# RMS norms' sums and rows moved to VectorE's 32x32 transposes, and half of the last residual turned there

## The chip, the cores and the metric

The kernel runs on one core of one Trainium2 chip. The metric is device time in microseconds (us), the median of three runs. The engines are TensorE (PE, with its weight loads as PEld), VectorE (DVE), ScalarE (ACT), GpSimd (POOL) and SyncE (SP, which here only issues DMAs). DMAs are issued by SP, POOL and ACT.

## What is computed

One hybrid layer on 1024 tokens of width 1024, in fp32:

```python
h = h + 0.5 * rmsnorm(swiglu(rmsnorm(h, ffn1_pre_g), ffn1_w_gu, ffn1_w_down), ffn1_post_g)
h = h + rmsnorm(hybrid_mixer(rmsnorm(h, mix_pre_g), w_in, ..., ssd_norm_g, attn_norm_g, w_out), mix_post_g)
h = h + rmsnorm(memory_cross_attention(rmsnorm(h, xa_pre_g), rmsnorm(mem, mem_g), xa_wq, xa_wkv, xa_wo), xa_post_g)
h = h + 0.5 * rmsnorm(swiglu(rmsnorm(h, ffn2_pre_g), ffn2_w_gu, ffn2_w_down), ffn2_post_g)
```

The mixer joins a stick-breaking attention and a Mamba-2 scan (SSD); the output of the scan is normed in two groups of channels before the output projection. An `rmsnorm` divides each token by the root of its mean square over the channels, and multiplies by a gain for each channel.

## The kernel before, in words

**Layout.** Activations lie with channels on the 128 partitions and tokens along a row. The tokens are two halves `hh` of 512, so a tensor of width 1024 is eight tiles of 128x512 for each half (`d` or `k` counts them). Only the last stage (`down_rows`) has tokens on partitions, since the output is stored so. Large products are split into high and low parts (`xh`, `xl`; `whi`, `wlo`) and done as three matmuls; the two FFNs use seven products of blocks instead of eight (`down7` for the second half of an FFN).

**Stages.** ffn1, the mixer's SSD part, its attention (heads in pairs, `p` from 0 to 7, the next pair's projection `inproj(p + 1)` merged in), `mix_out`, `xattn`, ffn2 with `down_rows` last.

**A norm.** Squares of the eight tiles are added into an accumulator `acc` of 128x512 (channels modulo 128 by tokens). Then the sum over partitions and what follows from it:

- `rms_cols` (L322): for each 128 tokens an fp32 matmul with `acc` as the stationary operand and a column of ones (`small`), into one column of a PSUM bank `ms`; then root (ACT) and reciprocal (DVE). It gives `c`, 128x4, with tokens on partitions. For the two SSD groups (`group_norm`, L1525) it works on the two `yacc` tiles together, for the memory (`keys`, L1548) on `Ct` of 256 columns.
- `rms_rows` (L346): for each of the four columns an fp32 matmul of the column, broadcast, with the identity, which puts each token's factor on all partitions; ACT copies the bank to a tile `r` of 128x512. `cpre`, `cpost`, `cy`, `cmem` are such columns, `rpre`, `rpost`, `rn` such rows.

`post` (L386) norms the output of a block, adds it to the residual `h` (also written to DRAM), and gathers the squares for the next norm; `pre` (L484) is that next norm alone. Some users take `c`, some take `r`, some both. `mix_row` and `memory_values` spread factors in the attention, `norm_row` (L2058) in `mix_out`.

**What sets the order.** A class records the program. `_pe` chains the matmuls in the order of the calls and adds an estimate of each to a `clock`. `later` is a list of steps with due times on that clock; a step due is called between two matmuls. In `pinned(t)` the matmuls float: they are placed behind the matmul at which the clock passes `t`. `kp` keeps an instruction in the order of the program on its engine. Elsewhere a scheduler orders DVE, ACT and POOL by priority, `urgent` raising it. Each engine and each queue works in order. The bank `ms` is one buffer, shared with transposes of the attention (`nb`).

**Attention, first pair.** `steps` (L1715) turns a half of v: DVE transposes, a store to DRAM (`vt`), four loads back (`dv<-vt`, L1731, 32x16x32 elements each). `kevac` stores k's high and low parts into `K` by SP DMAs (`k<-xl`, L1700), and `z<-k,q` multiplies with `K`.

**Last stage.** `down_rows` (L1140) takes eight tiles of the residual for each half (`fetch_h`, L1158, POOL). `shift` (L1160) turns them by 128x128 transposes on PE into two banks `mm`; `end` adds them to the normed result; `store` writes out. For the first half this is `early`, during the fifth and sixth product, for the second it is `last`, at the very end. `ssq` and `gain` gather squares and scale the rows. `blk<-h` (L685) are loads of residual tiles at the start of an FFN, from which DVE and ACT make the block sums (`wc`, `S`, `xl`) of its seven products.

Of the kernel before, what the change touches and what calls it, by code (L numbers as in the profile page):

```python
# [10 lines left out]
F32 = mybir.dt.float32  # L11
# [36 lines left out]
class Kern:  # L48
# [296 lines left out]

    def rms_rows(self, c, r, behind=None):  # L346
# [39 lines left out]
    def post(self, hh, gname, r2, gnext=None, out=None, step=None, spread=True, pins=(23000, 28000), accs=None, at=None, tail=None, hold=False, late=None):  # L386
# [10 lines left out]

        def cols():
            self.rms_cols([accs], c, r2=r2)

        def rows():
            self.rms_rows(c, r)
# [25 lines left out]
        if out is None:  # L428
            self.h[hh] = [self.tc.dram_tile([P, H], F32, name=self.nm(f"h{hh}{d}")) for d in range(KT)]
# [12 lines left out]
        if step is None:  # L442
            with self.pinned(T0 + t1):
                cols()
            with self.pinned(T0 + t2):
                rows()
# [19 lines left out]
        if out is None:  # L466
# [4 lines left out]
            self.held = [lambda: self.rms_cols([accs2], c2)]  # L471
            if not hold:
                q.append((t + t1, self.held.pop()))
            if spread:
                q.append((t + t2, lambda: self.rms_rows(c2[:, :], r2_)))
# [8 lines left out]
    def pre(self, hh, accs, t1, t2):  # L484
        c = self.t(self.rp, [P, 4], F32, f"cpre{hh}", bufs=2)
        r = self.t(self.rp, [P, H], F32, f"rpre{hh}", bufs=1)
        with self.pinned(t1):
            self.rms_cols([accs], c)
        with self.pinned(t2):
            self.rms_rows(c[:, :], r)  # L490
# [488 lines left out]
    def down1(self, sp, wdn, act_d, xs_d, gpost, gnext):  # L979
# [15 lines left out]
        def finish(m, i):  # L995
# [5 lines left out]
            elif m == 4:  # L1001
# [4 lines left out]
                self.post(0, gpost, self.C[0], gnext, step=2600, accs=accs[:], tail=(20500, 24000), late=38000)  # L1006
# [10 lines left out]
        self.post(1, gpost, self.C[1], gnext, step=2000, accs=accs[:], at=(6500, 9000, 10000), tail=(7500, 10500))  # L1017
# [122 lines left out]
    def down_rows(self, sp, wdn, act_d, xs_d, out):  # L1140
# [16 lines left out]
        def fetch_h(hh, d):  # L1157
            self.kp(nc.gpsimd.dma_start(out=hs[hh][d], in_=self.h[hh][d]))  # L1158

        def shift(hh, tb):  # L1160

            xt = [self.t(self.mmp, [P, H], F32, "mm") for _ in range(2)]
            for d in range(KT):
                self.tr(xt[d // 4][:, (d % 4) * P : (d % 4 + 1) * P], hs[hh][d][:, tb * P : (tb + 1) * P])
            return xt

# [34 lines left out]
        def early(tb):  # L1201

            root(0, tb)
            xt = shift(0, tb)
            for dh in range(2):
                end(0, tb, dh, xt)

        def finish(m, tb):
            if m == 2:
# [5 lines left out]
                for d in range(KT):  # L1215
                    at(2500 * d, fetch_h, 0, d)
            elif m == 4:
# [6 lines left out]
                for d in range(KT):  # L1224
                    at(1000 + 2500 * d, fetch_h, 1, d)
# [15 lines left out]
        def last(tb):  # L1241
            xt = shift(1, tb)
# [7 lines left out]
    def ssd(self, close):  # L1250

        nc, ap = self.nc, self.ap
        with self.tc.tile_pool(name=self.nm("ssa"), bufs=1, reuse_waits="tile") as ep, \
# [294 lines left out]
            def keys(n0, n1):  # L1548

                mh, ml, acc, rm = env["mem"]  # L1550
                if n0 == 0:
                    self.mem_c = self.t(self.rp, [P, 2], F32, "cmem")
# [94 lines left out]
    def attention(self):  # L1647
        nc, ap = self.nc, self.ap
        with self.pools("at", ["o", "a"], ["w"]) as (op, sp, wsp, pp):
# [52 lines left out]
            def inproj(p):  # L1702
# [12 lines left out]
                def steps(hh, t, before):  # L1715
# [14 lines left out]
                    for q in range(4):  # L1730
                        nc.sync.dma_start(  # L1731
                            out=v[32 * q : 32 * q + 32, :].rearrange("e (j c d) -> e j c d", j=4, c=4), in_=rows[q]
                        )
                    return v
# [49 lines left out]
                vtr(1, tv[1])  # L1784
                kevac(evac((yield from last), 1), h1)

            def before(n):
# [7 lines left out]
                if n == 10:  # L1795
                    late.append(mix_row(0))
                if n == 12:
                    late.pop()()
# [675 lines left out]
```

## Time and profile before

| | |
|---|---|
| median of three runs | 2584.47 us (2581.21 to 2585.56) |
| profiled execution, its own time | 2583.27 us |
| its span | 2581.5 us |
| mean granted TensorE clock | 0.999 |
| PE busy | 2564.0 us, 99% |
| DVE busy | 2000.7 us, 78% |
| ACT busy | 1289.0 us, 50% |
| POOL busy | 576.5 us, 22% |

The span runs from the first to the last instruction that the profiler recorded; the time of the execution has a little around it. A row of a group gives line, engine, operation, written tile `<-` read tiles, shapes and count; then total busy time and the mean of one in ns; then the idle time of the engine just before such an instruction, and whose end released it. A row of the timeline gives start, duration, engine, line, tiles and how many in a row, with idle time before it in brackets. An fp32 matmul shows as two PE instructions. Matmuls are pipelined, so the duration of one overlaps the next; what one costs is how far it moves the start of what follows.

### The profile page before, as it was taken

The numbers are of one execution on the slowest core, as the hardware profiler recorded it, in microseconds if no ns is written. First come the engines' busy times: TensorE is split into PE (matmuls) and PEld (weight loads), VectorE is DVE, ScalarE is ACT, GpSimd is POOL, SyncE is SP. The second block draws the span as 40 slices with busy tenths as digits, with TensorE's granted clock in tenths as the row PEclk, the third lists the DMA queues.
The fourth block names the chain that finished last, engine by engine and source line by source line (L and its number), as shares of the span: only waits on it lengthen the run. The fifth ranks groups of instructions, "written<-read, shape, count | busy, mean of one in ns | idle before, by whom it ended". The sixth has DMA issues, their size and how long they took to land. (4 is left out here: it accounts for less than half of the span.)

```text
span 2581.5 us, 36855 instructions
## 1 busy us (share of the span) xinstructions
PE 2564.0 (99%) x12786; PEld 2141.0 (83%) x12786; DVE 2000.7 (78%) x3074; ACT 1289.0 (50%) x2302; POOL 576.5 (22%) x674
## 2 busy tenths in 40 slices
PE   9999999999999999999999999999999999999999
PEld 7888888888787778888888898888888888888887
DVE  7988997779689884787787876876656887777777
ACT  7434444555356663555555654455554433334453
POOL 2555553001000001111111110111012655541000
PEclk9999999999999999999999999999999999999999
DMA  6458988655665516666666655547658443327654
GB/s 240 163 180 293 308 290 305 220 185 166 232 205 197 184 72 212 186 177 160 176 171 152 206 167 202 197 155 260 202 185 304 150 162 111 110 82 237 192 175 147
DMA packets 251628, 498.24 MB, mean 193 GB/s; under 512 B 60592, under 2 KB 69168, under 8 KB 251440
## 3 DMA queue, kind: packets, MB, share of 16 engines
q1 hardware_dynamic: 204176, 387.31, 46.4%
q0 software_dynamic: 23360, 65.03, 8.6%
q10 hardware_dynamic: 23904, 43.53, 4.6%
q8 instruction: 101, 1.65, 0.3%
q14 instruction: 87, 0.71, 0.1%
HBM read 331.65 MB, written 143.13 MB: 184 GB/s over the span
## 5 line engine op out<-in xcount | busy, mean ns | idle before, releaser
L139 PE MATMUL mm<-xh,whi 128*128 128x512 f32 x1312 | 516.7, 403 | 1.1 <-DVE ft L668 0.5
L139 PE MATMUL mm<-xh,wlo 128*128 128x512 f32 x1280 | 491.7, 392 | 0.0
L139 PE MATMUL mm<-xl,whi 128*128 128x512 f32 (+1 forms) x1248 | 485.7, 389 | 0.3 <-DVE xl L277 0.3
L139 PEld LDWEIGHTS mm<-xh,wlo 128*128 128x128 f32 x1280 | 240.6, 188 | 52.4 <-DVE wlo L270 0.5
L139 PEld LDWEIGHTS mm<-xh,whi 128*128 128x128 f32 x1312 | 247.0, 188 | 43.1 <-issue 3.9
L139 PEld LDWEIGHTS mm<-xl,whi 128*128 128x128 f32 x1248 | 235.6, 189 | 33.4 <-DVE xl L277 0.8
L1829 DVE TENSOR_TENSOR_SCAN nb<-nb,begin 128x128 f32<-128x128 f32 (+7 forms) x128 | 172.1, 1347 | 32.3 <-ACT nb L1825 31.9
L1825 ACT ACTIVATE nb<-z,scale 128x128 f32<-128x128 f32 (+2 forms) x192 | 109.5, 580 | 89.5 <-PE z L139 88.6
L270 DVE TENSOR_TENSOR wlo<-wraw,whi 128x1024 fp32r<-128x1024 f32 x61 | 74.6, 1223 | 51.3 <-ACT whi L268 50.9
L268 ACT CAST whi<-wraw 128x1024 fp32r<-128x1024 f32 (+1 forms) x77 | 73.9, 959 | 70.4 <-PE mm L139 43.5
L1846 POOL DMA_DIRECT2D mix<-sq x64 | 53.0, 828 | 248.7 <-DVE sq L1844 181.5
L669 ACT ACTIVATE ft<-ft 128x512 f32<-128x512 f32 x88 | 55.5, 632 | 95.5 <-DVE ft L668 94.9
L139 PE MATMUL dn<-xh,wlo 128*128 128x512 f32 x296 | 101.2, 390 | 0.0
L772 POOL TENSOR_TENSOR wc<-raw,wraw 128x512 f32<-128x512 f32 x55 | 80.7, 1467 | 56.4 <-DVE wlo L270 23.4
L268 ACT CAST ath<-tr 128x512 fp32r<-128x512 f32 (+1 forms) x106 | 57.3, 540 | 66.9 <-PE tr L142 61.9
L772 POOL TENSOR_TENSOR wc<-wraw,raw 128x512 f32<-128x512 f32 x56 | 78.9, 1409 | 52.5 <-DVE whi L270 16.5
L871 POOL TENSOR_TENSOR ft<-ft,e 128x512 f32<-128x512 f32 x37 | 59.7, 1614 | 126.3 <-DVE e L867 51.1
L270 DVE TENSOR_TENSOR atl<-tr,ath 128x512 fp32r<-128x512 f32 (+1 forms) x106 | 66.1, 625 | 28.0 <-ACT ath L268 26.9
L139 PE MATMUL mm<-ath,v 128*128 128x256 f32 x320 | 87.8, 297 | 0.0
L139 PE MATMUL dn<-xh,blk 128*128 128x512 f32 x264 | 85.2, 389 | 0.0
L268 ACT CAST wlo<-wc 128x512 fp32r<-128x512 f32 x79 | 49.1, 621 | 69.2 <-PE dn L139 25.4
L139 PE MATMUL mm<-atl,v 128*128 128x256 f32 x320 | 83.1, 282 | 0.0
(601 smaller groups left out, 6795.2 us busy)
## 6 DMA issues: line engine op xcount, KB each, us to landing
whi<-dwhi SPq DMA_DIRECT2D x82, 512.0 KB, 4.1
wlo<-dwlo SPq DMA_DIRECT2D x82, 512.0 KB, 5.4
wraw<-in_w_gu SPq DMA_DIRECT2D x43, 512.0 KB, 4.0
dwhi<-bh SPq DMA_DIRECT2D x78, 256.0 KB, 4.2
dwlo<-bl SPq DMA_DIRECT2D x78, 256.0 KB, 4.2
raw<-in_w_gu SPq DMA_DIRECT2D x37, 512.0 KB, 4.1
wraw<-xs SPq DMA_DIRECT2D x56, 256.0 KB, 2.9
xs<-ft ACTq DMA_DIRECT2D x54, 256.0 KB, 3.0
```

Of the source, the lines that this page charges most:

```text
L139: self._pe(self.nc.tensor.matmul(out, lhsT, rhs, start=start, stop=stop, skip_group_check=self.more), cost)
L268: self.kp(self.nc.scalar.copy(hi, src))
L270: self.nc.vector.tensor_tensor(out=lo, in0=src, in1=hi.bitcast(F32), op=ALU.subtract)
L669: nc.scalar.activation(t, t, AF.Silu)
L772: inst = (nc.vector if early else nc.gpsimd).tensor_tensor(out=t, in0=a, in1=b, op=op)
L871: nc.gpsimd.tensor_tensor(out=t1, in0=t1, in1=e, op=ALU.mult)
L1825: nc.scalar.activation(nb[:, s0:s1], z[:, 0:n], AF.Sigmoid, scale=sc[:, i : i + 1])
L1829: nc.vector.tensor_tensor_scan(out=nb[:, 0:Wd][:, ::-1], data0=nb[:, 0:Wd][:, ::-1], data1=begin[:, S - Wd : S][:, ::-1], initial=0.0, op0 ...
L1846: nc.gpsimd.dma_start(out=self.mix_d[p][a * 64 : a * 64 + 64, csl], in_=o, accum_op=ALU.add)
```

## The change

**Sums by DVE.** A new function `turned` takes over from `rms_cols`: DVE transposes the accumulator in place in blocks of 32x32, so that tokens (32 of each block) lie on partitions and channels in the row; a DVE reduce adds each block's 32 columns into `part` (128x16); one fp32 matmul with `onesr`, now a matrix of ones at places equal modulo 32, adds the four groups of 32 partitions and leaves the sum in each group; ACT takes the root into `root` (128x16), DVE the reciprocal. Where a user wants `c`, POOL copies it together by four copies of 32x4.

**Rows by ACT and DVE.** A new function `spread` takes over from `rms_rows`: ACT copies `root` broadcast to 128x512, DVE transposes it in place in 32x32 blocks.

Both are used for ffn1's next norm of both halves, the two SSD groups with `mix_row` and `norm_row`, the memory, the mixer's posts and the first half's next norm, and both posts and next norms of the cross-attention. The first norm, ffn1's own posts, the attention's output norm and the mixer's held next norm of the second half stay as they were. Some due times and pins move by 1 to 1.5 us.

**Last stage.** The first half's residual is read by 32 DMAs on POOL in 128-byte pieces (`fetch_rows`), so that 32x32 blocks lie right for a DVE transpose (`turn`), 15 us later by the clock; `early` then needs no PE transposes. To give these DMAs one source, the eight `h` tiles are views of one DRAM tensor `hall[hh]`. The second half stays with PE transposes, but its first squares and gains come later.

**Attention, first pair.** The four loads of v's second half come after the stores of k's second half.

```diff
+    def turned(self, accs, ms, wait, c=None, out=None):
+        ps = self.t(self.msp, [P, H], F32, "ms", bufs=1)
...
+        for i, acc in enumerate(accs):
...
+            self.kp(nc.vector.transpose(acc, acc))
+            self.kp(nc.vector.tensor_reduce(out=part, in_=acc.rearrange("p (j k) -> p j k", k=32), op=ALU.add, axis=mybir.AxisListType.X))
+            pin = self.pinned(self.clock + wait) if chains else nullcontext()
+            with pin:
+                self.mm(ps[:, 16 * i : 16 * i + n], self.one, part, True, True)
+        for i, x in enumerate(roots):
+            self.kp(nc.scalar.activation(x, ps[:, 16 * i : 16 * i + n], AF.Sqrt, bias=self.eps, scale=ms))
+            self.kp(nc.vector.reciprocal(x, x))
+        if c is not None:
+            for q in range(4):
+                k = slice(32 * q, 32 * q + 32)
+                nc.gpsimd.tensor_copy(c[k], roots[0][k].rearrange("p (b q) -> p q b", q=4)[:, q])
...
+    def spread(self, root, r):
+        x = r[:, 0 : 32 * root.shape[1]]
+        self.kp(self.nc.scalar.copy(x.rearrange("p (j k) -> p j k", k=32), root.unsqueeze(2).to_broadcast([P, root.shape[1], 32])))
+        self.kp(self.nc.vector.transpose(x, x))
...
-            self.pre(hh, accs2, T0 + pins[0], T0 + pins[1])
+            self.pre(hh, accs2, T0 + pins[0], T0 + pins[1], turn[1])
...
-                c = self.norm_c[gr] = self.t(self.rp, [P, 8], F32, f"cy{gr}")
-                self.rms_cols([[y] for y in yacc], c, ones=self.ones512)
+                self.norm_c[gr] = self.turned(yacc, 1.0 / 512.0, 3000)
...
-                    self.rms_cols([[acc]], self.mem_c)
+                    self.turned([acc], 1.0 / D_MODEL, 2500, out=self.mem_c)
...
-                        self.rms_rows(self.mem_c[:, :], rm)
+                        self.spread(self.mem_c, rm)
...
+        def fetch_rows(tb, dh, behind):
+            self.kp(nc.gpsimd.tensor_copy(self.scratch, behind[:, 0:1]))
+            rows = self.hall[0].rearrange("(h k) (c e) t -> h e (k c) t", h=2, e=32)[dh]
+            x = hs[0][2 * tb + dh]
+            for q in range(4):
+                t = tb * P + 32 * q
+                out = x[32 * q : 32 * q + 32, :].rearrange("e (c t) -> e c t", t=32)
+                self.kp(nc.gpsimd.dma_start(out=out, in_=rows[:, :, t : t + 32]))
+
+        def turn(tb, dh):
+            x = hs[0][2 * tb + dh]
+            self.kp(nc.vector.transpose(x, x))
...
-            xt = shift(0, tb)
             for dh in range(2):
-                end(0, tb, dh, xt)
+                end(0, tb, dh, hs[0][2 * tb : 2 * tb + 2])
...
+            if m < 4:
+                C = (self.F[0][1::2], self.F[1][1::2], self.F[1][0::2], self.F[0][0::2])[m]
+                for dh in range(2):
+                    at(1000 + 6000 * dh, fetch_rows, m, dh, C[2 + dh])
+                    at(16000 + 6000 * dh, turn, m, dh)
...
-                for d in range(KT):
-                    at(2500 * d, fetch_h, 0, d)
...
-                    at(3000 + 5000 * tb, ssq, 1, tb, 0)
-                    at(5000 + 5000 * tb, gain, 1, tb, 0)
+                    at(6500 + 3800 * tb, ssq, 1, tb, 0)
+                    at(8500 + 3800 * tb, gain, 1, tb, 0)
...
-                vtr(1, tv[1])
+                if p:
+                    vtr(1, tv[1])
                 kevac(evac((yield from last), 1), h1)
+                if p == 0:
+                    vtr(1, tv[1]())
```

The order on PE at the mixer's first post, before. `dn` is the output projection's bank; the four matmuls of `ms` are the sums of the post, 128 tokens each.

```order
L139 MATMUL dn_16584<-xh_1386_6374,wlo_16547 128x512
L139 MATMUL dn_16584<-xh_1387_6375,whi_16546 128x512
L139 MATMUL ms_16589<-small_114,acc_3486_16033 128x1 x4
L139 MATMUL dn_16584<-slo_16261,whi_16546 128x512
L139 MATMUL dn_16584<-xh_1387_6375,wlo_16547 128x512
```

And now, in the same place; `part` is what DVE has reduced, `onesr` the matrix of ones.

```order
L139 MATMUL dn_16569<-slo_16493,whi_16511 128x512
L139 MATMUL dn_16569<-xh_1391_6381,wlo_16512 128x512
L139 MATMUL ms_16554<-part_4_79,onesr_121 128x16
L139 MATMUL dn_16569<-xh_1392_6382,whi_16511 128x512
L139 MATMUL dn_16569<-slo_16497,whi_16511 128x512
```

One matmul of 16 columns stands where four of one column stood, further on in that product, and the group of four with `ident` and `cpost` that followed is gone.

The order on SP in the attention's first pair, before: `k` is a part of K, `dv` a turned half of v.

```order
L1700 DMA k_9855<-xl_2197_9851 64x512
L1731 DMA dv_10059<-vt_10057 32x16x32 x4
L1700 DMA k_9855<-xl_2198_9852 64x512
L1700 DMA k_9856<-xl_2197_9851 64x512
L1700 DMA k_9856<-xl_2198_9852 64x512
```

And now:

```order
L1776 DMA k_9845<-xl_2185_9841 64x512
L1776 DMA k_9845<-xl_2186_9842 64x512
L1776 DMA k_9846<-xl_2185_9841 64x512
L1776 DMA k_9846<-xl_2186_9842 64x512
L1809 DMA dv_10049<-vt_10047 32x16x32 x4
```

The four loads of v stand behind all stores into K.

The order on POOL at the start of ffn2, before: `h<-F` are the last writes of the residual, `blk<-h` the first loads of its tiles.

```order
L416 DMA h_4311_19684<-F_4290_19592 128x512
L416 DMA h_4312_19685<-F_4293_19625 128x512
L416 DMA h_4313_19686<-F_4295_19652 128x512
L685 DMA blk_20031<-h_4108_18779 128x512
L685 DMA blk_20031<-h_4310_19683 128x512
L685 DMA blk_20034<-h_4306_19679 128x512
L685 DMA blk_20034<-h_4112_18783 128x512
L685 DMA blk_20084<-h_4109_18780 128x512
```

And now; `cpre` is the second half's column of factors, made from `root`.

```order
L474 DMA h_4264_19617<-F_4249_19534 128x512
L474 DMA h_4264_19617<-F_4251_19563 128x512
L474 DMA h_4264_19617<-F_4253_19590 128x512
L371 COPY cpre_4282_19697<-root_6_81 32x4 x4
L746 DMA blk_19956<-h_4075_18730 128x512
L746 DMA blk_19956<-h_4264_19617 128x512
L746 DMA blk_19959<-h_4264_19617 128x512
L746 DMA blk_19959<-h_4075_18730 128x512
```

Four copies, which wait for the second half's root, stand between the writes and the loads.

More of the change, by code (lines that the diff above doesn't have):

```diff
@@ L384, in resid, with post @@
         self.later += [(self.clock + start + step * d, lambda d=d: one(d)) for d in range(KT)]
-    def post(self, hh, gname, r2, gnext=None, out=None, step=None, spread=True, pins=(23000, 28000), accs=None, at=None, tail=None, hold=False, late=None):
+    def post(self, hh, gname, r2, gnext=None, out=None, step=None, spread=True, pins=(23000, 28000), accs=None, at=None, tail=None, hold=False, late=None, turn=(False, False)):
         nc = self.nc
@@ L442, in post @@
         if step is None:
-            with self.pinned(T0 + t1):
+            with self.pinned(T0 + t1 + 1500):
                 cols()
-            with self.pinned(T0 + t2):
-                rows()
+            rows()
             for d in range(KT):
@@ L487, in pre @@
         with self.pinned(t1):
-            self.rms_cols([accs], c)
-        with self.pinned(t2):
-            self.rms_rows(c[:, :], r)
+            root = self.turned(accs, 1.0 / D_MODEL, 0, c)[0] if turn else self.rms_cols([accs], c)
+        if turn:
+            self.spread(root, r)
+        else:
+            with self.pinned(t2):
+                self.rms_rows(c[:, :], r)
         self.R[hh], self.C[hh] = r, c
@@ L1729, in steps, with back @@
                     rows = o.rearrange("(c e) (j q d) -> q e j c d", c=4, q=4, d=32)
[L1730 to L1734, printed above, removed]
+                    def back():
+                        for q in range(4):
+                            nc.sync.dma_start(
+                                out=v[32 * q : 32 * q + 32, :].rearrange("e (j c d) -> e j c d", j=4, c=4), in_=rows[q]
+                            )
+                        return v
+                    return back if hh and p == 0 else back()
                 def vtr(hh, t):
@@ L2059, in norm_row @@
                 r = self.t(rp, [P, H], F32, f"rn{i}")
[L2060 to L2061 removed]
+                if i < 2:
+                    self.spread(self.norm_c[i][hh], r)
+                else:
+                    with self.pinned(self.clock + at):
+                        self.rms_rows(self.norm_c[i][:, 0:4], r)
                 return r
@@ L2110, in mix_out @@
                     self.run_later(float("inf"))
-                    self.post(0, "mix_post_g", None, "xa_pre_g", step=5000, spread=False, accs=ends[0], at=(6000, 11500, 14000), tail=(18000, 0))
+                    self.post(0, "mix_post_g", None, "xa_pre_g", step=5000, spread=False, accs=ends[0], at=(6000, 11500, 14000), tail=(18000, 0), turn=(True, True))
                     self.resid(1, 5000, 17000)
@@ L2114, in mix_out @@
                     self.flush(0)
-                    self.post(1, "mix_post_g", None, "xa_pre_g", step=3000, spread=False, accs=ends[1], at=(6000, 10500, 13000), hold=True)
+                    self.post(1, "mix_post_g", None, "xa_pre_g", step=3000, spread=False, accs=ends[1], at=(6000, 10500, 13000), hold=True, turn=(True, False))
     def xattn(self):
@@ L2297, in run @@
             self.place(tp, 64)
-            self.place(cp, 448)
+            self.turns = 0
+            self.place(cp, 128)
+            self.part = [self.t(x, [P, 16], F32, f"part{n}") for n, x in enumerate((cp, rp))]
+            self.roots = [self.t(cp, [P, 16], F32, f"root{n}") for n in range(4)]
             self.params = self.t(cp, [P, NPAR], F32, "params")
```

96 lines of the change are left out of this document (66 added, 30 removed).

## The prediction

> **What bounds the kernel now.** I read the page's first two lines first: the span, and each engine's busy time.
>
> ```profile
> span 2581.5 us, 36855 instructions
> PE 2564.0 (99%) x12786; PEld 2141.0 (83%) x12786; DVE 2000.7 (78%) x3074; ACT 1289.0 (50%) x2302; POOL 576.5 (22%) x674
> ```
>
> TensorE (PE) is busy for 2564.0 of 2581.5 us, so 17.5 us are all that it idles, first loads and last stores included. VectorE (DVE) is busy 78%, ScalarE (ACT) 50%, GpSimd (POOL) 22%. Time is gained here by taking instructions off PE, or by ending its few waits; work given to another engine is free as long as PE does not come to wait for it. Next I read the waits of PE. The two longest, by engine, line and what was waited for (total, times, longest):
>
> ```profile
> PE z L139 <- DMA k<-xl: 1.9, 1, 1.9
> PE ms L139 <- DVE atl L270: 1.9, 1, 1.9
> ```
>
> Last I read the groups by line and shape, for the small matmuls that the change touches: sums of squares over partitions (small against an accumulator), rows spread over partitions (identity against four columns), and transposes of the last stage's residual (xh, xl).
>
> ```profile
> L139 PE MATMUL ms<-small,acc 128*128 128x1 f32 x104 | 12.4, 241 | 0.2 <-DVE acc L369 0.2
> L139 PE MATMUL ms<-ident,cpre 128*128 128x128 f32 x48 | 6.4, 277 | 0.0
> L139 PE MATMUL ms<-ident,cpost 128*128 128x128 f32 x48 | 6.3, 274 | 0.0
> L142 PE MATMUL mm<-ident,xh 128*128 128x128 f32 x32 | 4.9, 274 | 0.0
> L142 PE MATMUL mm<-ident,xl 128*128 128x128 f32 x32 | 4.8, 272 | 0.0
> L139 PE MATMUL ms<-small,yacc 128*128 128x1 f32 x32 | 3.8, 248 | 0.0
> L139 PE MATMUL ms<-ident,cy 128*128 128x128 f32 x16 | 2.2, 281 | 0.0
> L139 PE MATMUL tr<-ident,cy 128*128 128x128 f32 x16 | 2.1, 274 | 0.0
> L139 PE MATMUL ms<-ident,cmem 128*128 128x128 f32 x8 | 1.3, 287 | 1.9 <-DVE atl L270 1.9
> L139 PE MATMUL ms<-small,Ct 128*128 128x1 f32 x4 | 0.5, 229 | 0.0
> ```
>
> Idle time ahead of them is next to nothing: they stand between large matmuls on a busy PE, so what they take, PE loses. The duration of one overlaps its neighbours', so I price them by what they push back.
>
> **The change part by part.** *Price of a small group.* From the timeline of PE at the end of the mixer, a group of sums and a group of rows, eight instructions each (four fp32 matmuls, two instructions apiece):
>
> ```profile
> 1602.81 0.40 PE L139 MATMUL dn<-xh,whi 128*128 128x512 f32 x1
> 1603.04 0.95 PE L139 MATMUL ms<-small,acc 128*128 128x1 f32 x8
> 1603.86 0.48 PE L139 MATMUL dn<-slo,whi 128*128 128x512 f32 x1
> 1604.17 0.40 PE L139 MATMUL dn<-xh,wlo 128*128 128x512 f32 x1
> ...
> 1609.62 0.39 PE L139 MATMUL dn<-xh,wlo 128*128 128x512 f32 x1
> 1609.85 1.05 PE L139 MATMUL ms<-ident,cpost 128*128 128x128 f32 x8
> 1610.66 0.48 PE L139 MATMUL dn<-xh,whi 128*128 128x512 f32 x1
> 1610.97 0.39 PE L139 MATMUL dn<-slo,whi 128*128 128x512 f32 x1
> ```
>
> Large matmuls start 0.23 us apart (1609.62 to 1609.85, with the group behind). From 1602.81 to 1604.17 are 1.36 us with two of them, so the sums cost 1.36 - 0.46 = 0.90 us; from 1609.62 to 1610.97 likewise 1.35 - 0.46 = 0.89 us for the rows. That is 0.112 us an instruction.
>
> *Removed.* Sums: of acc's 104 instructions four groups of eight stay (two at the start, ffn1's first post, the held one after mix_out), so 72 go, with all 32 of yacc and 4 of Ct: 108. Rows: 32 of cpre's 48 and 32 of cpost's go (the start's and ffn1's posts stay), with 32 of cy and 8 of cmem: 104. Transposes: half of 64, the first half of the tokens: 32. The last I price like the rows, by the shape they share. Together 244 x 0.112 = 27.3 us.
>
> *Added on PE.* 14 matmuls (128x16, fp32) against the quads of ones, two instructions each: 28 x 0.112 = 3.1 us by the rows above, between whose 1 and 128 columns its 16 lie. Net: 24.2 us off PE.
>
> *The two waits.* First the attention's, with SP's queue beside it and PE's clock after it (window, busy time of PE, PEld, DVE, ACT, POOL, then the granted clock):
>
> ```profile
> 1037.90 0.36 PE L139 MATMUL z<-k,q 128*128 128x256 f32 x1 [1.93 <-DMA k<-xl]
> ...
> 1038.68 0.63 PE L139 MATMUL mm<-xl,whi 128*128 128x512 f32 x1
> 1039.11 0.63 PE L139 MATMUL mm<-xh,wlo 128*128 128x512 f32 x1
> ```
> ```profile
> 1032.62 2.63 SPq L1731 DMA_DIRECT2D dv<-vt  x4
> 1035.35 1.86 SPq L1700 DMA_DIRECT2D k<-xl  x3
> ```
> ```profile
> 1037.80:1041.40 3.60, 3.50 (x10) 3.03 (x11) 2.75 (x4) 1.74 (x4) 0.00 (x0) 0.55 0.87 224
> ```
>
> Three loads of k stood behind four of dv, which took SP 2.63 us to issue. The change puts the dv loads behind k, so k comes about 2.6 us earlier and the 1.93 us go. Its v half comes about 1.9 us later, behind three k loads, and its splits are not urgent yet. After the wait the clock stood at 0.55 for 3.6 us, and large matmuls came 0.43 us apart in place of 0.23: 0.45 x 3.6 = 1.6 us more. Together 3.5 us. [...]
>
> The second wait, in the attention's last part:
>
> ```profile
> 1497.82 0.49 PE L142 MATMUL ms<-ident,nb 128*128 128x128 f32 x3
> 1500.18 0.71 PE L139 MATMUL ms<-ident,cmem 128*128 128x128 f32 x4 [1.87 <-DVE atl L270]
> ```
>
> The cmem rows need the one ms bank, which DVE is still reading. With the spread on ACT and DVE no such matmul exists; the next on PE are products whose inputs are there. I take off 1.9 us.
>
> *Added elsewhere.* For DVE and ACT the nearest rows:
>
> ```profile
> L1725 DVE STREAM_TRANSPOSE dv<-dv 128x512 f32<-128x512 f32 x16 | 11.2, 700 | 0.3
> L2165 DVE TENSOR_REDUCE st<-dn 128x1 f32<-128x256 f32 x32 | 13.4, 420 | 7.7 <-PE dn L139 7.6
> L355 ACT COPY rpost<-ms 128x512 f32<-128x512 f32 x6 | 3.5, 588 | 10.8 <-PE ms L139 10.8
> ```
>
> DVE gets 14 + 14 transposes for the norms and 8 in the last stage, 36 x 0.70 = 25.2 us, and 14 reduces of 512 columns at 0.7 (0.42 for 256; between 0.42 and 0.84), 9.8 us. DVE goes from 2000.7 to about 2036 us, 80% of a shorter span. ACT's broadcast copy takes the place of a copy of the same size: nothing. The cover is DVE's idle fifth, and the lead of the accumulators over PE's pinned place. Where I laid DVE's order beside PE's times, most of the 14 part matmuls have over 3 us in hand; the mixer's first post at about 1607 us has none, for its matmul is pinned 2.5 us behind sums that DVE puts between other work. If cover is gone, one site costs 0.5 to 2 us and perhaps half clock. I allow 1.5 us in all (0 to 10).
>
> *Queues moved.* POOL gets five sets of four small copies (32x4). The one that matters is at ffn2's start, ahead of the first blk loads:
>
> ```profile
> 1950.73 3.71 POOL L685 DMA_DIRECT2D blk<-h  x7 [0.31 <-DMA whi<-dwhi]
> 1966.33 1.32 ACT L688 ACTIVATE blk<-blk,params 128x512 f32<-128x512 f32 x2
> 2001.29 0.68 DVE L270 TENSOR_TENSOR S<-wc,S 128x512 fp32r<-128x512 f32 x1
> 2019.27 2.88 PE L139 MATMUL dn<-S,whi 128*128 128x512 f32 x12
> ```
>
> The copies wait for the root, which I estimate at about 1962.5 us by its place in the order of PE, so the loads go out 12 us later and land near 1968 to 1972 instead of before 1966.33. The chain of block sums that they feed ends at 2001.29 and is first multiplied at 2019.27: a delay of 2 to 6 us is covered. I cost it at nothing; what hides it is those 18 us. Behind the other four sets stand loads and stores whose users are farther off by the order.
>
> *Last stage.* In place of 8 plain loads POOL issues 32 of 64 KB in 128-byte pieces, and DVE turns them 15 us later, in order. Nearest rows are the same pattern on SP (count, size, median us to landing) and POOL's loads of 256 KB:
>
> ```profile
> dv<-vt SPq DMA_DIRECT2D x64, 64.0 KB, 2.6
> xl<-h POOLq DMA_DIRECT2D x32, 256.0 KB, 5.5
> 2376.00:2476.00 100.00, 100.00 (x443) 82.74 (x442) 77.54 (x126) 51.95 (x93) 3.22 (x6) 1.00 0.67 211
> ```
>
> Four in a row land after 2.6 to 22 us (4 x 5.5, if each waited for the last). I take 6, by the same pattern; POOL works 3.2 us of these 100 and DVE has 22 free for 5.6 us of turning. Each set of loads follows a POOL copy that waits for a result tile F, to pace them; behind it on POOL stand only the next loads and late stores. Cost nothing, cover gone beyond 15 us. The later squares of the second half are ACT and DVE work ahead of an unchanged end.
>
> *Sum.* The profiled execution took 2583.3 us (1.8 around its span), 1.2 below the median of 2584.5. 2583.3 - 24.2 - 3.5 - 1.9 + 1.5 = 2555.2; for the median 1.2 more, 2556.4: **2556**.
>
> **The rivals.** *DVE late at several sites.* For it: in the attention's tail, at 1607 us and in the second cross-attention post DVE is already dense and its queue runs in order, so a turn waits its place and PE waits at the part matmul, 1 to 2 us a time, some with half clock. Against it: margins elsewhere are long. Five sites at 1.5 us and two half-clock stretches of 1.6 are 11 us less the 1.5 allowed: 2565. Chance 0.15.
>
> *POOL's copies hold ffn2's loads too long.* For it: 12 us later issue. Against it: the 18 us above. If it eats them, PE waits about 5 us and loses 1.6 to the clock: 2563. Chance 0.04.
>
> *Nothing gained from small matmuls*, if PE's saved time turned into waits for the weights that stream in behind. Only the two waits then count: 2584.5 - 3.5 - 1.9 = 2579, right at the bound of same. Against it: the DMA share is 0.67 even in the dense stretch above, and no wait of PE names weights. Chance 0.02.
>
> *Slower: the turned residual comes late.* DVE stands in order at each turn until four piecewise loads have landed; splits of weights and blocks queue behind, then PE waits. Each of eight turns that makes PE wait w costs w + 1.6 (half clock). The 28 us forecast as gained are gone when w passes 28/8 - 1.6 = 1.9 us, thus from a landing of 17 us, plus the lead that DVE has; at w = 4, 8 x 5.6 = 45 us: 2601. For it: 22 us is the far end of my bound, and nothing of before loads such pieces through POOL. Against it: 2.6 us of the same pieces on SP, and POOL empty. Chance 0.04, of which 0.03 is slower by more than can be told apart. [...]
>
> **How the numbers follow.** Forecast 0.75 (2552 to 2561: 216 instructions fewer at 0.10 to 0.12 us are 2 us either way, new waits 0 to 6). Rivals one and two beside it, 0.19, reach to 2567 with the 10 us that is the far end of the allowance. Below, 2549 holds a day on which the runs fall 3 us low, as the lowest of before did (2581.2). So the range is 2549 to 2567; the ends of the rivals and the last two cases are left out. A measurement of this kernel tells about 0.2%, 5 us, from no change: faster than 2579.3 holds the forecast, the first two rivals and half of the third, 0.95; same 0.02; slower 0.03.
>
> **What would show it.** In the profile after: PE's busy time near 2540 with the groups cy, yacc, Ct, cmem gone and acc, cpre, cpost at 32, 16, 16; no wait for k<-xl at 1036 and clock 1.00 there; DVE near 2036. Waits of PE on part show the first rival; a gap before 2019 the second; DVE's waits for xh<-h or xl<-h the last. I am wrong if PE's busy time falls by less than 20 us, or its idle time rises above 17.5.

## The result and the profile after

| | before | changed |
|---|---|---|
| median, same chip | 2584.81 us (6 runs, 2580.79 to 2585.95) | 2568.32 us (6 runs, 2565.0 to 2572.5) |
| ratio | | 0.994 [0.9928, 0.9953] |
| profiled execution, span | 2583.27, 2581.5 us | 2569.24, 2567.5 us |
| PE busy, idle | 2564.0, 17.5 us | 2542.9, 24.6 us |

The kernel is 16.5 us faster. I had forecast 28 (2556, range 2549 to 2567), so the direction is right and the size is not: by the medians 12 us are missing, and in the profiled execution, on which the accounts below rest, 14.0. The page of the changed kernel, its first two lines:

```profile
span 2567.5 us, 36544 instructions
PE 2542.9 (99%) x12570; PEld 2116.0 (82%) x12570; DVE 2031.7 (79%) x3128; ACT 1291.8 (50%) x2305; POOL 599.8 (23%) x726
```

PE has 216 instructions fewer, as counted, and DVE is at 2032 us (forecast 2036). But PE idles 24.6 us, where 15.2 followed from my sum; over 17.5 was my own sign of being wrong. The groups of PE and DVE that the change touches:

```profile
L139 PE MATMUL ms<-part,onesr 128*128 128x16 f32 x26 | 3.9, 238 | 0.9 <-DVE part L358 0.9
L139 PE MATMUL ms<-small,acc 128*128 128x1 f32 x32 | 3.9, 242 | 0.0
L139 PE MATMUL ms<-ident,cpre 128*128 128x128 f32 x16 | 2.2, 281 | 0.0
...
L356 DVE STREAM_TRANSPOSE acc<-acc 128x512 f32<-128x512 f32 x9 | 6.4, 707 | 0.1
L358 DVE TENSOR_REDUCE part<-acc 128x16 f32<-128x512 f32 x9 | 6.1, 680 | 0.2
```

In 28 instructions PE waited once for `part`, 0.9 us: the place that I had watched is nearly innocent. The waits of PE (total, times, longest) show what it waits for instead:

```profile
PE dn L139 <- ACT F L1177: 2.5, 1, 2.5
PE dn L139 <- DVE wlo L270: 1.9, 1, 1.9
PE mm L139 <- DMA wlo<-dwlo: 1.8, 1, 1.8
PE mm L139 <- DVE ft L729: 1.4, 1, 1.4
...
PE ms L139 <- DVE part L358: 0.9, 1, 0.9
PE mm L139 <- DVE wlo L270: 0.9, 1, 0.9
...
PE mm L139 <- ACT k L268: 0.7, 1, 0.7
PE mm L139 <- DVE k L270: 0.5, 1, 0.5
...
PE dn L139 <- DVE pt L270: 0.5, 1, 0.5
```

`k<-xl` and the wait ahead of cmem are gone. The first row was there before with 1.3 us, and the profiles of all runs have from 0.33 to 2.81 for it. New are operands that the change does not touch: low parts of weights (`wlo`), the cross-attention's `k` (a slot that its last output weights use) and probabilities (`pt`). Where the idle time sits is read from the windows. A row gives the stretch, its length, then the busy time (and count) of PE, PEld, DVE, ACT and POOL, then the granted clock, the busy share of the DMA engines and their GB/s; PE's idle time is the length less PE's busy time. Two windows, the mixer's output with its posts (1530 to 1700) and the cross-attention (1700 to 1960), of the kernel before:

```profile
1530.00:1700.00 170.00, 170.00 (x824) 143.08 (x823) 122.33 (x183) 72.73 (x112) 12.29 (x23) 1.00 0.62 207
1700.00:1960.00 260.00, 259.98 (x1297) 218.48 (x1296) 175.68 (x355) 146.76 (x271) 32.70 (x61) 1.00 0.65 216
```

and of the changed kernel:

```profile
1530.00:1700.00 170.00, 167.19 (x758) 138.36 (x757) 129.82 (x193) 75.58 (x114) 12.74 (x25) 0.99 0.59 196
1700.00:1960.00 260.00, 257.71 (x1250) 213.95 (x1249) 181.78 (x364) 145.85 (x272) 34.15 (x68) 1.00 0.66 221
```

Before, PE idled 0.02 us here in all; now it idles 2.81 and 2.29 us. The other stretches, worked out in the same way: 0 to 660 us (start, ffn1) 5.3 before, 7.8 after; 660 to 1020 (SSD) 1.0 and 1.9; 1020 to 1430 (attention) 1.9 and 2.0, where 0 was expected; 1430 to 1530 2.6 and 1.6, where 0.7 was; 1960 to the end 6.6 and 6.2.

The longest new wait has half clock behind it, at the mixer's second post. The first matmul, and the window behind it with the granted clock third from the end:

```profile
1641.15 0.70 PE L139 MATMUL dn<-ohi,wlo 128*128 128x512 f32 x1 [1.87 <-DVE wlo L270]
```
```profile
1641.10:1644.50 3.40, 3.35 (x8) 2.71 (x9) 3.40 (x5) 0.00 (x0) 0.00 (x0) 0.53 0.91 287
```

Eight matmuls in 3.4 us: in this execution the 1.6 us of half clock that the change ends at 1038 (the granted clock from 1037.80 to 1041.40 is 1.00 now, and was 0.55) come back here.

### The profile page after: what moved, and what is told of

Read it like the earlier page. It is cut to its first block, busy times and chain, and to the rows that moved or that the text cites. A ratio compares the mean times of both kernels' runs of the same rounds, so it can differ in the third digit from the quotient of the medians.

```text
span 2567.5 us, 36544 instructions
## 1 busy us (share of the span) xinstructions
PE 2542.9 (99%) x12570; PEld 2116.0 (82%) x12570; DVE 2031.7 (79%) x3128; ACT 1291.8 (50%) x2305; POOL 599.8 (23%) x726
```

## The experiments

Theory after the result: (1) DVE's added work delays the splits that share its queue. Rivals: (2) PE, 216 instructions shorter, reaches operands sooner than ACT and DVE can make them (pace); (3) the scheduler, which orders ACT and DVE by its own estimate of times, places splits worse when PE's instructions are gone (order). "Local" below means that the same PE matmuls of two profiles are laid beside each other in time, ahead of a place and behind it: what the difference grows by was lost or gained there. All times are in us; before is the kernel before on the same chip.

| run | median | before | ratio |
|---|---|---|---|
| e1_last | 2580.63 | 2584.25 | 0.9988 [0.9979, 0.9996] |
| e2_dve | 2585.59 | 2584.25 | 1.0004 [0.9995, 1.0013] |
| e3_vold | 2569.07 | 2584.25 | 0.9943 [0.993, 0.9957] |
| e4_noasum | 2566.99 | 2584.25 | 0.9934 [0.9922, 0.9947] |
| e5_xaold | 2571.12 | 2582.57 | 0.9949 [0.9936, 0.9961] |
| e6_mixold | 2567.95 | 2582.57 | 0.994 [0.9927, 0.9952] |
| e7_ssdold | 2572.83 | 2582.57 | 0.9958 [0.9945, 0.9972] |
| e8_try | 2571.41 | 2582.57 | 0.995 [0.9937, 0.9962] |
| e9_peonly | 2565.92 | 2585.29 | 0.9925 [0.9911, 0.9939] |
| e10_try2 | 2567.78 | 2585.29 | 0.9936 [0.9923, 0.9948] |
| e11_fill | 2568.09 | 2585.00 | 0.994 [0.9928, 0.9953] |
| e12_try3 | 2566.97 | 2585.00 | 0.9931 [0.9918, 0.9945] |
| e13_pace8 | 2570.23 | 2583.47 | 0.9948 [0.9935, 0.996] |
| e14_pace4 | 2570.11 | 2583.47 | 0.9948 [0.9934, 0.9961] |
| e15_kfirst | 2568.50 | 2584.15 | 0.9945 [0.9931, 0.9959] |
| e16_try4 | 2566.28 | 2584.15 | 0.9937 [0.9925, 0.995] |

**e1_last: the last stage alone.** The kernel before with `fetch_rows`, `turn` and the later squares and gains.

```diff
-            xt = shift(0, tb)
...
+                    at(1000 + 6000 * dh, fetch_rows, m, dh, C[2 + dh])
+                    at(16000 + 6000 * dh, turn, m, dh)
```

> The kernel before with the change of the last stage alone (residual of the first half read in 128-byte pieces and turned by DVE, later squares of the second half). If the step was costed rightly, 32 PE transposes go (3.6 us) and nothing waits in their place, with the 0.8 us gap near 2544 us gone as in the changed kernel: 4.3 us faster than before, 2577 in the profile. If the lost gain went here (turns late, splits behind them on DVE), it is 0 to 2 us faster and the profile has new waits of PE after 2343 us.

Measured 3.6 less at the median, 1.3 in the profiles, whose last wait (for F, 1.95 us at 2539.55, the granted clock being 0.72 from 2539 to 2545) is one that varies over the profiles, from 0.75 (before) to 3.74 (e8), with the old last stage and the new. At the median the last stage earns what its 32 instructions cost, though the interval leaves 1 to 5 us open; its profile shows no wait for the turned residual. The miss is looked for elsewhere.

**e2_dve: DVE's work alone.** The kernel before; each accumulator is also transposed twice, behind its sums, and each row passed through a maximum with itself. PE keeps all its work.

```diff
+                    for _ in range(2):
+                        self.kp(nc.vector.transpose(acc, acc))
...
+                self.kp(nc.vector.tensor_tensor(out=r, in0=r, in1=r, op=ALU.max))
```

> The kernel before with the change's work on DVE added and nothing taken off PE: each accumulator that the change turns is transposed twice in place after its sums are taken (it is not read again until rewritten), each row tile goes once through a DVE maximum with itself. About 30 us more on DVE, values unchanged. Theory 1 (DVE, crowded and in order, hands PE its split operands late): new waits of PE in the mixer's output (1595 to 1660 us) and in the second half of the cross-attention (1835 to 1900 us), 4 to 9 us slower than before in all. Theory 2 (the order of queues and engines was reshuffled, load itself is harmless): within 1.5 us of before and no new waits at those places.

DVE busy 2027.8, 27.1 more than before, and no change of time. Its two windows:

```profile
1530.00:1700.00 170.00, 170.00 (x830) 143.39 (x830) 128.80 (x193) 73.84 (x114) 12.32 (x23) 1.00 0.62 207
1700.00:1960.00 260.00, 259.99 (x1297) 218.28 (x1296) 182.04 (x365) 146.95 (x271) 32.84 (x61) 1.00 0.65 213
```

DVE is as busy as in the changed kernel (128.8 and 182.0) and PE idles in neither window. So DVE's added load alone does not make the waits. In the mixer ACT and DVE also keep the order of the kernel before there, but for the added instructions.

**e9_peonly: PE's work alone.** The kernel before without the sums and rows on PE: ACT takes the factors from a slice of the accumulator, so these norms are not computed. DVE stays at 2000.8.

```diff
+                self.kp(nc.scalar.activation(c[:, g * n : g * n + n], accs[0][:, 0:n], AF.Sqrt, bias=self.eps))
...
+                self.kp(nc.scalar.copy(x, c.unsqueeze(2).to_broadcast([P, nb, P])))
```

> The kernel before with the same sums and rows taken off PE as by the change, and nothing put on DVE in their place: the factors are made by ACT from a slice of the accumulator (so the sums over partitions are left out, and the norms are wrong there). 212 small PE instructions less are 23.7 us, the wait for the ms bank 1.9 us: 25.6 us faster than before, 2556 in the profile, if a shorter PE alone brings no new waits. If the waits near 988, 1444 to 1449, 1598, 1641 and 1828 to 1892 us are there as in the changed kernel (about 9 us), a PE that arrives sooner is enough to make them, whatever DVE has to do more. If they are not there, they need both: work off PE and work on DVE.

Span 2564.1: 17.4 shorter (19.4 at the medians), not 25.6. PE idles 23.0 in all, where the kernel before idles 17.5 and the changed one 24.6. Its two windows:

```profile
1530.00:1700.00 170.00, 169.55 (x776) 140.91 (x775) 128.73 (x200) 78.00 (x122) 12.80 (x23) 1.00 0.57 194
1700.00:1960.00 260.00, 256.75 (x1233) 212.69 (x1232) 174.16 (x345) 145.58 (x268) 33.42 (x62) 1.00 0.68 229
```

In the cross-attention PE waits 3.25 us with no DVE work added. So taking instructions from PE is enough there; but ACT's and DVE's orders move with it, so this does not tell pace from order. In the attention's end there are waits for xl at 1444 and 1447 (1.1), as in the changed kernel. In the mixer 0.45 are left, at the wait for wlo:

```profile
1635.57 0.50 PE L139 MATMUL dn<-ohi,wlo 128*128 128x512 f32 x1 [0.45 <-DVE wlo L270]
```

From 1603 to 1645 the order on ACT and DVE here is that of the changed kernel, and not that of the kernel before.

**e5_xaold, e6_mixold, e7_ssdold: one part old.** The changed kernel with the norms of the cross-attention, of the mixer's posts, or of the SSD groups and the memory as before.

```diff
-                    self.post(0, "xa_post_g", None, "ffn2_pre_g", step=5000, at=(8500, 16000, 19000), turn=(True, True))
+                    self.post(0, "xa_post_g", None, "ffn2_pre_g", step=5000, at=(8500, 16000, 19000))
...
```

> The changed kernel with both cross-attention posts and their next norms in the old way (sums and rows on PE). PE gets 56 instructions back, 6.3 us. If the small waits of PE between 1828 and 1892 us (3.5 us together in the changed kernel) come from the new norm at this place, they go, and the kernel is 2.8 us slower than the changed one. If they come from an order reshuffled elsewhere, they stay: 6.3 us slower.

> The changed kernel with both posts of the mixer in the old way. PE gets 34 instructions back, 3.8 us. If the waits at 1598 us (part, about 1 us) and 1641 us (DVE's wlo, 0.7 to 2.0 us and at times 1.7 us of half clock) come from the new norm at this place, they go: 2 us slower to 1 us faster than the changed kernel. If they stay: 3.8 us slower. The waits from 1828 us on should not change by either theory.

> The changed kernel with the norms of the two SSD groups and of the memory in the old way. PE gets 66 instructions back, 7.4 us, and the wait for the ms bank near 1500 us, 1.9 us. If the waits near 988 us (DVE's wlo, 1.1 to 1.4 us), 1444 to 1449 us (1.8 us) and 1514 us (0.55 us) come from these norms, they go: 5.7 us slower than the changed kernel. If they come from elsewhere: 9.3 us slower.

Local, by stage: e5 ends the waits from 1828 to 1892 and is 2.65 later behind that stage; e6 ends those at 1598 and 1641 and is 0.8 earlier, so in these two profiles the mixer's posts gave nothing; e7 is 2.9 later from 640 to 1700, not 5.7, since waits at 988, 1444 to 1449, 1514, and those at 1598 and 1641 too, go with the edit (the half clock at 1641 as well: the granted clock is 1.00 in 1530 to 1700, but 0.98 in 1430 to 1530, where the changed kernel has 1.00). By the ratios e5 is 2.3 and e7 4.6 slower than the changed kernel and e6 the same, with 3 to 4 either way. What the norms take off PE comes back in part as waits near the edit and, as e7 shows for 1641, 100 us further on.

**e4_noasum: less DVE work in the mixer.** The changed kernel without the 14 adds of the attention's output norm, which is then taken from one tile.

```diff
-                    nc.vector.tensor_tensor(out=asum[-1], in0=asum[-1], in1=sq, op=ALU.add)
```

> The changed kernel without the 14 DVE additions that gather the squares of the attention's output in the mixer's output stage (so that norm is taken from one tile of eight; part of the computation left out). Theory 1: with about 10 us of DVE work gone from 1600 to 1760 us, the wait for DVE's wlo near 1641 us goes and with it its half clock: 3.5 us faster than the changed kernel, the rest unchanged. If that wait is not DVE's load but the order or the weights' DMA, it stays: no difference.

The wait at 1641 and its half clock go (the granted clock in 1530 to 1700 is 1.00, for 0.99), idle time in 1530 to 1700 falls from 2.81 to 0.27, and the stage ends 4.4 earlier (local). The profiled run lost that elsewhere; the median is 1.3 below the changed kernel's, which its interval does not tell from none. The edit takes DVE work away and changes DVE's order at once, so it does not tell load from order.

**e3_vold: the swap of v and k undone.** The changed kernel with the four dv loads ahead of k, as before.

```diff
-                if p:
-                    vtr(1, tv[1])
+                vtr(1, tv[1])
                 kevac(evac((yield from last), 1), h1)
-                if p == 0:
-                    vtr(1, tv[1]())
```

> The changed kernel with the reload of v's second half back in its old place, so that SP's queue has its old order there. Theory 2 for this place (the move put the loads of the next weights behind the q stores on SP): the waits for whi<-dwhi and wlo<-dwlo near 1056 us (2.0 us and the spacing behind them) go, the wait for k<-xl near 1034 us comes back, 1.9 us with 1.6 us of half clock: 1 to 1.5 us slower than the changed kernel. If the wait at 1056 us came from DVE instead, it stays, and the kernel is 3.5 us slower.

The same time as the changed kernel. The wait for k is back, but without the half clock behind it (the wait, then its window with the granted clock of 1.00):

```profile
1035.42 0.36 PE L139 MATMUL z<-k,q 128*128 128x256 f32 x1 [2.33 <-DMA k<-xl]
```
```profile
1035.40:1038.80 3.40, 3.38 (x19) 3.02 (x20) 2.83 (x5) 2.36 (x6) 0.00 (x0) 1.00 0.88 208
```

And the wait for `wlo` at 1058 is gone. That wait is what the swap brought, as PE and SP's queue of the changed kernel show:

```profile
1057.92 0.50 PE L139 MATMUL mm<-xh,wlo 128*128 128x512 f32 x1 [1.76 <-DMA wlo<-dwlo]
```
```profile
1043.18 0.34 SPq L212 DMA_DIRECT2D braw<-in_w_out  x1
...
1050.46 0.59 SPq L182 DMA_DIRECT2D whi<-dwhi  x1
1051.10 0.54 SPq L182 DMA_DIRECT2D wlo<-dwlo  x1
```

In the kernel before, whi and wlo were issued at 1041.68 and 1042.22; now braw, dwhi, dwlo and q stand ahead of them, and they go out at 1050.46 and 1051.10.

**e11_fill, e13_pace8, e14_pace4: work put back.** The changed kernel with useless small matmuls on PE in the cross-attention's first post: four columns and four rows (16 instructions), eight columns (16), four columns (8). In e13 and e14 the order on ACT, DVE, POOL and SP is that of the changed kernel. The lines are e13's.

```diff
+                for b in range(8 if fill else 0):
+                    self.mm(ps[:, 64 + b : 65 + b], acc[:, b % 4 * P : (b % 4 + 1) * P], self.ones, True, True)
```

> The changed kernel with useless work put back on PE at one place: in the first half's cross-attention post, four matmuls as the old sums and four as the old rows, whose results nobody reads (16 instructions, 1.8 us by the price of 0.112). The order on DVE, ACT, POOL and SP is that of the changed kernel. If PE waits there because it comes sooner to operands that are made at the same pace as before, the work costs nothing: the waits from 1828 to 1892 us shrink by 1.8 us in all, and the kernel takes the time of the changed one within 0.3 us up to 1960 us. If PE is the bound there, it is 1.8 us slower and the waits stay.

> The changed kernel with eight useless matmuls of one column (16 instructions, 1.8 us by the price of 0.112) behind the part matmul of the first half's cross-attention post; the order on ACT, DVE, POOL and SP is held to that of the changed kernel in every place. Pace: the waits from 1828 to 1892 us (2.3 us of idle PE between 1700 and 1960 us) shrink by about what the work takes, and PE is at the same place at 1900 us within 0.5 us. Order: the waits stay, and everything behind comes 1.8 us later.

> The same with four useless matmuls (8 instructions, 0.9 us), and the changed kernel's order on ACT, DVE, POOL and SP in every place without being held. Pace: the idle time between 1700 and 1960 us falls by about 0.9 us and nothing comes later. Order: 0.9 us later, idle time as before.

In e11 PE idles 0.15 in 1700 to 1960, not 2.29, and stands 1.3 earlier at 1910 against the changed kernel than at 1700, though it has 1.8 more to do. But its order moved, in some 50 places on ACT and 85 on DVE, against what its expectation says. With the order held, e13 is 1.4 later at 1890 than at 1700 and idles 2.14; e14 is 1.2 later and idles 2.37; the waits on pt, ol and k from 1866 to 1889 all stay, each within 0.05 of its length. A PE that comes 1.2 to 1.4 later does not end them, so pace falls for this place; what e11 changed is the order. ACT's splits of k and whi in e11, then in e13 (whose lines stand 6 further down):

```profile
1885.30 1.05 ACT L268 CAST k<-wraw 128x1024 fp32r<-128x1024 f32 x1
1886.87 1.05 ACT L268 CAST whi<-wraw 128x1024 fp32r<-128x1024 f32 x1 [0.51 <-PE mm L139]
```
```profile
1883.03 1.05 ACT L274 CAST whi<-wraw 128x1024 fp32r<-128x1024 f32 x1 [1.58 <-PE mm L145]
...
1885.55 1.05 ACT L274 CAST k<-wraw 128x1024 fp32r<-128x1024 f32 x1
```

The same two rows of the kernel before, and of the changed one:

```profile
1889.69 1.05 ACT L268 CAST k<-wraw 128x1024 fp32r<-128x1024 f32 x1
1891.26 1.06 ACT L268 CAST whi<-wraw 128x1024 fp32r<-128x1024 f32 x1 [0.52 <-PE mm L139]
```
```profile
1884.26 1.05 ACT L268 CAST whi<-wraw 128x1024 fp32r<-128x1024 f32 x1 [1.59 <-PE mm L139]
...
1886.78 1.06 ACT L268 CAST k<-wraw 128x1024 fp32r<-128x1024 f32 x1
```

PE needs k first. Before, k came first; now ACT waits for a slot to split whi, copies results, and splits k 0.7 us too late.

**e15_kfirst: that one order turned round.** The changed kernel with k's split tied ahead of whi's and of two copies: 8 places in ACT's order, 2 in DVE's; the orders of POOL and SP are the same, and so is PE's program.

```diff
+                if hh and len(self.F[hh]) < 2:
+                    self._after(x.ins, self.k_split[0])
...
+                    if d == 0:
+                        for x, y in zip(self.k_split, self.last_split):
+                            self._after(y, x)
```

> The changed kernel with one order turned round at the end of the cross-attention: the split of k (high part on ACT, low part on DVE) stands ahead of the split of the next output weights (whi, wlo) and of the first two copies of the product into F, as it did before the change; 8 places in ACT's order and 2 in DVE's differ, PE's, POOL's and SP's orders are the same. Theory that the order on ACT and DVE makes the waits: in the changed kernel ACT casts whi, which PE needs at 1894, at 1884.3, and k, which PE needs at 1887.2, only at 1886.8; with k first it is done before 1886.6, the waits of 0.70 and 0.53 us on k at 1888 and 1889 go, PE idles about 1.0 us in 1700 to 1960 in place of 2.29, and the products behind stand 1.2 us earlier against the changed kernel than they stand at 1880. Rival, that PE simply comes too early for what ACT and DVE can do: the waits stay or move to F or whi within the next 10 us, and the shift at 1940 is within 0.3 us of that at 1880. In the whole run 1 us is too little to be told apart.

PE, and its window over the cross-attention:

```profile
1885.16 0.50 PE L139 MATMUL mm<-oh,k 128*128 128x512 f32 x1
```
```profile
1700.00:1960.00 260.00, 258.66 (x1250) 214.48 (x1249) 183.42 (x365) 144.82 (x269) 34.28 (x68) 1.00 0.68 226
```

The two waits on k are gone, idle time is 1.34, 0.95 less, and PE is 1.0 earlier behind the place than ahead of it (local). For the waits on k, order is shown as the cause. In the whole run 1 us can't be told, as expected.

**e8_try, e10_try2, e12_try3, e16_try4: a better version?** e8 reloads v's half through POOL in its old place and raises the priority of all weight splits; e10 raises it only from the mixer's output to the cross-attention and pins `part` 2 us later in the mixer; e12 raises it only in the mixer's output and for k; e16 is e12 with the order of e15. e10 and e12 also have e8's reload, e12 also the later pin. The lines are e10's.

```diff
-            self.split(hi, lo, raw)
+            with self.urgent() if self.late_splits else nullcontext():
+                self.split(hi, lo, raw)
...
+                            (nc.gpsimd if hh and p == 0 else nc.sync).dma_start(
```

> An attempt at a better version: the changed kernel with the four loads of v's second half of the first pair issued by POOL in their old place, so that SP's queue has neither them ahead of K nor the weights behind q; and with the splits of weight tiles raised in priority on ACT and DVE. If order is what costs, the waits near 1034 and 1056 us go (2.3 us), the one at 1641 us (0.7 to 3.7 us), and those for the k split near 1887 us (1.5 us): 4 to 7 us faster than the changed kernel. If load on DVE is what costs, the waits only move to other operands: within 2 us of the changed kernel.

> A second attempt at a better version: as the first (v's reload on POOL, weight splits raised in priority), but the priority only in the mixer's output and the cross-attention, and the matmul on part pinned 4.5 us behind the sums in the mixer's posts in place of 2.5. The start should be as in the changed kernel again (3.0 us better than the first attempt), the wait at 1598 us (1.8 us there) gone; against the changed kernel 4 to 6 us faster if nothing new comes late.

> A third attempt at a better version: as the second, but the raised priority of weight splits only in the mixer's output and for the one k split, since the second attempt shows new waits of 2.1 us between 1711 and 1748 us, where the weight splits stand ahead of pt. These should go, and the rest stay as in the second attempt: 5 to 6 us faster than the changed kernel by 2500 us.

> The variant e12_try3 (reload of v through POOL in its old place, weight splits in the mixer's output and k's split raised in priority, the mixer's part matmuls 2 us later) with the same order as in e15_kfirst: k ahead of whi and of the copies into F. By the theory of order it is 0.7 us shorter than e12_try3, so about 2566 us where the changed kernel takes 2568 to 2570; by the rival the same as e12_try3. A gain of 2 to 3 us on the changed kernel is at the edge of what five rounds tell.

In all four the wait at 1641 is gone, and e10 and e16 idle 0.01 in 1530 to 1700; e12 waits 0.90 for `part` at 1671. Raised everywhere, the splits stand ahead of the first norm's squares and cost 3.0 at the start (e8); raised in the cross-attention, they bring 1.45 of new idle time from 1705 to 1755 and put PE 2.6 later there (e10, local). In e16 the waits on k are gone as in e15, and PE is 0.6 earlier behind them against e12, where 0.7 was expected. e16 has the lowest median, 2566.28, and e12 the lowest ratio of the four, 0.9931, but the interval of each holds the changed kernel's ratio of 0.994. The 4 to 7 us that were expected of e8, e10 and e12 did not come, and none of the four is shown to be faster.

## Why the prediction was right and wrong

**Right.** PE is the bound, and most of what leaves it is gained. 244 instructions went and 28 came. The price holds where nothing waits: over ffn1's two next norms (652 to 700) 28 instructions fewer put PE 3.1 us earlier (0.111 each, for 0.112). DVE's rows are as costed (0.71 and 0.68 us for 0.70 and 0.70). The wait ahead of cmem is gone. ffn2's loads and the last stage hid, as costed at nothing; the latter's loads (their tiles are named `xh` and `xl`) land, at the median, in

```profile
xh<-h POOLq DMA_DIRECT2D x16, 64.0 KB, 3.9
xl<-h POOLq DMA_DIRECT2D x16, 64.0 KB, 4.3
```

and not in the 17 us from which the slower rival decided; no wait of DVE between 2343 and 2510 names them.

**Wrong: "I allow 1.5 us in all (0 to 10)" for new waits.** Idle time of 15.2 followed from the sum, and 24.6 came: 9.4 of the miss of 14.0 (2569.2 for 2555.2), of which 2.0 belong to the swap below. The step behind it was "most of the 14 part matmuls have over 3 us in hand". That held, but it answers the wrong question: I asked whether DVE is late for `part`. What came late were splits of weights and probabilities that the change does not touch. Taking the instructions off PE is enough for most of it: PE idles 23.0 in e9, with no work added on DVE, while e2, with DVE's load alone, has no wait in the mixer's output or the cross-attention.

How a shorter PE brings them is shown at k alone: ACT's and DVE's orders are made anew when PE's program is shorter, and turning one place back ends the waits (e15). At 1641 three kinds of edit end the wait: less DVE work (e4), the old sums (e6, e7), raised priority (e8, and with the later pin e10, e12, e16). Order is likely there too: with the old order there is no wait, DVE's load or not (before, e2), and with the new one there is, DVE's load or not (changed, e9). But its size is not the order's alone: seven profiles have the same order on PE, ACT, DVE and POOL in the mixer's output (changed, e3, e5, e11, e13, e14, e15), and in them it runs from 0.55 (e3) to 2.67 (e13). So the 0.45 of e9 does not tell whether DVE's load lengthens it. No run turned the order at 1641 alone: order is not shown there.

The waits in the SSD part and the 2.5 us more at the start were not taken apart further. At the start a wait for F near 475 moves by 2 us between profiles, but 0.9 are the change's: a wait for `ft` near 29 us takes 1.40 or 1.41 in every profile of the changed kernel and its variants and 0.47 or 0.48 in every one built on the kernel before. Why stays open.

**Wrong: "Together 3.5 us" for the swap of k and v.** The wait for k went and one of 1.76 us for wlo came (with one of 0.23 for whi ahead of it), since on SP the loads of weights fell back behind braw and the stores of q. I named the loads that the v half is moved past, and not those that fall behind as SP's queue shifts: e3, without the swap, takes the same time. The 1.6 us of half clock in the sum do not come with every such wait: in the window behind the wait for k the granted clock was 0.55 in before and 0.60 in e1 (1037.90 to 1041.30), but 1.00 in e3, whose wait was longer (2.33 for 1.93).

**Mis-sized: PE's busy time.** It fell by 21.1, not by 24.2 + 1.6, which is 4.7 of the miss. 1.6 are the half clock at 1641, which of those seven profiles only this one and e15 have (the granted clock in 1530 to 1700 is 0.99 in these two and 1.00 in the other five). The other 3.1 make 21.1 / 216 = 0.098 an instruction; e9, with a mean granted clock of 0.999 as before and the changed kernel have, gives 22.9 / 212 = 0.108. The matmul right behind a wait shows 0.50 us (at 1057.92) for 0.39, and at half clock 0.70 (at 1641.15) for 0.63; whether waiting is booked there as busy, and how much of the 3.1 that would be, stays open.

**The rivals.** "DVE late at several sites" (2565, chance 0.15) came nearest in time and was only half right in cause: one wait of 0.9 us on `part`, and the rest on other operands, most of which come late without DVE's added work too (e9). A rival in which operands that the change does not touch come late was missing.

## What to carry to other kernels

When work is taken off the bound engine, list every operand that it reads in that stretch with the time by which it is ready, and not only those that the change makes: the removed work was their cover. Where a scheduler sets the order, an edit on one engine reorders the others; compare their orders around each place before pricing, and look for an operand that is needed sooner standing behind one that is needed later. Of a load that is moved in a queue, follow also what is pushed back behind the new head.

## What the runs showed of the hardware

Half clock does not follow the length of a wait alone. Behind 1.93 us at 1038 (before) and 1.87 us at 1641 (changed) the granted clock was 0.55 and 0.53 for some 3.5 us; behind 1.76 us at 1058 (changed), 1.87 us at 1500 (before) and 2.33 us at 1035 (e3) it stayed at 1.00. The window of the changed kernel behind the wait at 1058, and that of before behind the wait at 1500:

```profile
1057.90:1061.30 3.40, 3.38 (x20) 2.98 (x21) 0.98 (x2) 1.21 (x3) 1.20 (x5) 1.00 0.90 294
```
```profile
1500.10:1503.50 3.40, 3.32 (x27) 3.32 (x28) 1.74 (x3) 1.03 (x3) 0.00 (x0) 1.00 0.16 41
```

What tells the two kinds apart was not shown. A wait of about 2 us cost 1.6 us more here (0.45 x 3.6 at 1038, 0.47 x 3.4 at 1641) or nothing, so such a cost belongs in a sum as a chance, not as a fixed term.
